# The heads' stage of a gated-linear-attention layer: DMAs, casts and evacuations in written order on every engine

## The chip, the cores and the metric

The kernel runs on one core of one Trainium2 chip. The metric is the device time of one execution in microseconds (us). The kernel before takes 2637.93 us, the median of three runs (2637.6 to 2638.26).

## What is computed

The reference is a two-layer step of a streaming encoder over 512 frames of one new stream (the prompt) and 16 frames each of eight running streams (the samples): 640 tokens of width 2048. Layer 0 is stick-breaking attention with a key and value cache, layer 1 is gated linear attention (GLA) with a recurrent state; both are preceded by a normalization with shift and scale from a condition, and gated. The change lies in layer 1, whose core is this chunk, run for four heads with DK = 256 and DV = 512:

```python
def gla_chunk(S, inp):
    q, k, v, g = inp                       # g = log of the decay, per token and key column
    b = jnp.cumsum(g, axis=1)
    b_last = b[:, -1]
    q_in = q * jnp.exp(b)
    a = jnp.einsum('bchd,bshd->bhcs', q_in, k * jnp.exp(-b))
    a = jnp.where(jnp.tril(jnp.ones((C, C), dtype=bool)), a, 0.0)
    o = jnp.einsum('bhcs,bshe->bche', a, v) + jnp.einsum('bchd,bhde->bche', q_in, S)
    S = jnp.exp(b_last)[..., None] * S + jnp.einsum('bshd,bshe->bhde', k * jnp.exp(b_last[:, None] - b), v)
    return S, o
...
g = jax.nn.log_sigmoid(a_lr @ w_a2 + b_a) / 16.0
o = o * lax.rsqrt(jnp.mean(o * o, axis=-1, keepdims=True) + EPS) * g_out
y = (o * jax.nn.silu(r)) @ w_out
```

The outputs are the encoded frames of both kinds, the new keys and values of layer 0, and the new states of layer 1: 4 of 256 x 512 for the prompt and 32 of them for the eight samples.

## The kernel before

Everything is float32. Large products are made of three products of halves: a value is split by `halves` (lines 134 to 136) into a rounded high part, cast on ScalarE (L135), and a low part, subtracted on VectorE (L136).

The stages follow one another: layer 0's condition and first values (to about 200 us), its input projections (L520, to 955), its attention (to 1450), its output product and layer 1's condition and first values (to 1700), layer 1's input projections (L520 again, to 2086), the heads' stage (lines 1288 to 1676, to 2510), and the last output products with the final norm (lines 1679 to 1748).

**The heads' stage** runs several strands side by side. TensorE's order is written out by the program (line 81), by a small clock `pe["now"]` that each matmul moves on. A strand is a generator, a *lane*; `step(wait, tp=n)` says that it goes on once that many microseconds of this clock have passed and n PSUM banks are free. Between pieces of the filler work, `side.tick()` (L305) runs the lanes that are due. The filler is first the plain projection of the queries and keys of heads 2 and 3 (`plain`, L575: 16 pieces of weights, 48 matmuls each), then two of the four groups of output products (`share`, L619: rows 0 to 3 and 4 to 7 of the gated output, times w_out). The lanes are:

- `decays` (L1397): for each head, loads q, k and the decay's weights, makes the cumulated log decays b on ScalarE and VectorE, and scales q and k by their exponentials. Two heads can be ready ahead.
- `prompt_lane` (L1451): 16 chunks of 128 tokens. For each: scores and turned keys kr (L1357, L1500), scores times values (`mm3`, L1345), queries times the state, which is scaled and split into S1h and S1l (L1472, L1473) once for each half of the key columns, then the norm (`normed`: L1369, the power on GpSimd L230, the scaling L1371), then the state's update. The turning back of the normalized chunk and its gating (`leave`, L1389, L1390) come in the next chunk.
- `sample_lane` (L1557): for each head, the eight samples at once. The keys times the decay (kd) are turned (L1585), split, stored to DRAM as two tiles (L1589) and read back by 12 loads of 16 rows x 4 x 128 (L1595) into kst, where high part, high part and low part stand below each other, 48 rows for each of two samples, so that one matmul of 128 rows makes the update of one sample (L1619). Then come four groups of four states: queries times states (L1613), four updates (L1619, L1621), and the states' stores.
- `fetches` (L1631): loads the gated rows of both lanes from DRAM, splits them (ogh, ogl) and so frees the output products to start: rows 0 to 13 here, 14 and 15 in the last stage.

**Who issues DMAs.** `load` and `store` go on SyncE's queue (L71, L74), `move` on GpSimd's (L78). Here SyncE has the weights, q, k, the values v and the rows; GpSimd has the state tiles s0 in and out (eight buffers, L1546, L1554), gates, values of the sample lane (vst), the plain projection's results, the gated results og, and the stacked keys. A DMA waits on its queue for what it reads or overwrites, and those behind it wait too.

**What sets the order.** In this stage only TensorE follows the program text. The order of VectorE, ScalarE, GpSimd and SyncE's queue is chosen at build time by a scheduler that simulates the program; in an earlier stage (lines 1161 to 1275) VectorE, ScalarE and GpSimd follow the text too.

## Time and profile before

| | us |
|---|---|
| median of three runs | 2637.93 |
| the profiled execution, its own time | 2633.23 |
| its span in the trace | 2631.4 |
| TensorE busy in the span | 2475.0 |
| VectorE busy | 1597.8 |
| ScalarE busy | 1017.4 |
| GpSimd busy | 261.3 |

The profile is of one execution. Its page gives busy times by engine; the windows give the same for a stretch of time, with TensorE's granted clock (1.00 is full speed), the mean busy share of the 16 DMA engines and their rate. In the list of waits, a row is the waiting engine, what it writes and its line, then what it waited for, the sum in us, the number of waits and the longest. "issue" is time in which nothing shows that the engine waited for. In the timeline, a row is the start, the time, the engine, line, instruction, what is written from what, its shape and how many; an idle time before it and its end are in brackets. PE is TensorE, PEld its weight loads, DVE VectorE, ACT ScalarE, POOL GpSimd, SPq SyncE's queue.

### The profile page before, as it was taken

What the parts mean: (1) busy time and instruction counts of PE and PEld (TensorE: products, weight loads), DVE (VectorE), ACT (ScalarE), POOL (GpSimd) and SP (SyncE); (2) the same over time, 40 slices, a digit from 0 to 9 for tenths busy, and PEclk for the clock granted to TensorE, in tenths of its full rate; (3) what the DMA queues carried; (4) which work ended last, traced back from release to release, by engine and by line L of the source; (5) the groups of instructions that cost most, each with busy time, mean ns of one, the idle gap of its engine ahead of it and who ended that gap; (6) DMA issues with size and microseconds to landing.
All of it is one profiled execution on the core that took longest, in us unless ns stands there. A gap on an engine that the chain in (4) does not pass through costs nothing.

```text
span 2631.4 us, 43839 instructions
## 1 busy us (share of the span) xinstructions
PE 2475.0 (94%) x17393; PEld 2162.9 (82%) x17393; DVE 1597.8 (61%) x2429; ACT 1017.4 (39%) x1804; POOL 261.3 (10%) x537
## 2 busy tenths in 40 slices
PE   6999999999999989999999989999999998787998
PEld 4569999989999989787777767999999987675776
DVE  4555556555556646766776666666677564555556
ACT  4332222222223335555453453333333362464333
POOL 1200000000000000000000050000000134424300
PEclk8899999999999999999999989999999998999999
DMA  9966666766674366666665633344543577846554
GB/s 314 314 208 222 216 216 202 232 209 216 198 237 144 118 215 212 227 209 221 209 225 173 189 110 108 90 119 117 144 119 105 170 226 233 280 158 209 203 196 148
DMA packets 495358, 503.83 MB, mean 191 GB/s; under 512 B 26090, under 2 KB 416626, under 8 KB 495026
## 3 DMA queue, kind: packets, MB, share of 16 engines
q1 hardware_dynamic: 477426, 446.49, 53.7%
q0 software_dynamic: 17728, 54.54, 6.3%
q8 instruction: 137, 2.24, 0.3%
q14 instruction: 67, 0.55, 0.1%
HBM read 411.16 MB, written 89.78 MB: 190 GB/s over the span
## 4 chain that ended last, share of the span: by engine, by line
PE 74%; DMA 7%; DVE 7%; issue 5%; ACT 3%; POOL 3%; SPq 1%; ACTq 0%; POOLq 0%; DVEq 0%
PE ps_mm L520 41%; PE ps_mm L619 8%; PE ps_mm L454 4%; PE ps_mm L356 3%; PE ps_mm L575 3%; PE ps_tp L976 2%; PE ps_tp L944 1%; PE ps_z L920 1%; PE ps_z L178 1%; DMA ar<-in_w_ada_dram 1%; PE ps_z L218 1%; DVE wl L136 1%; PE ps_tp L1021 1%; PE ps_mm L1747 1%; PE ps_z L989 1%
## 5 line engine op out<-in xcount | busy, mean ns | idle before, releaser
L520 PE MATMUL ps_mm<-sums,wh 128*128 128x320 f32 x2880 | 642.2, 311 | 0.4 <-ACT wh L135 0.4
L520 PE MATMUL ps_mm<-h,wh 128*128 128x320 f32 x2160 | 484.7, 313 | 5.5 <-ACT wh L135 3.8
L520 PEld LDWEIGHTS ps_mm<-sums,wh 128*128 128x128 f32 x2880 | 479.4, 188 | 12.2 <-issue 9.0
L520 PE MATMUL ps_mm<-sums,wl 128*128 128x320 f32 x1440 | 445.3, 309 | 0.7 <-DVE wl L136 0.7
L520 PEld LDWEIGHTS ps_mm<-h,wh 128*128 128x128 f32 x2160 | 360.4, 188 | 22.0 <-issue 13.3
L136 DVE TENSOR_TENSOR wl<-wr,wh 128x1024 fp32r<-128x1024 f32 x191 | 233.9, 1226 | 234.0 <-ACT wh L135 233.0
L135 ACT CAST wh<-wb 128x1024 fp32r<-128x1024 f32 x180 | 188.9, 1049 | 460.2 <-PE ps_mm L520 389.6
L520 PE MATMUL ps_mm<-h,wl 128*128 128x320 f32 x1080 | 334.8, 310 | 2.2 <-DVE wl L136 2.2
L135 ACT CAST wh<-wr 128x1024 fp32r<-128x1024 f32 x191 | 200.1, 1049 | 330.4 <-PE ps_mm L520 201.1
L520 PEld LDWEIGHTS ps_mm<-sums,wl 128*128 128x128 f32 x1440 | 270.4, 188 | 1.0 <-DVE wl L136 1.0
L136 DVE TENSOR_TENSOR wl<-wb,wh 128x1024 fp32r<-128x1024 f32 x180 | 219.9, 1222 | 66.0 <-ACT wh L135 63.4
L619 PE MATMUL ps_mm<-wh,ogh 128*128 128x512 f32 x450 | 199.7, 444 | 15.5 <-ACT ogh L135 11.0
L575 PE MATMUL ps_mm<-h,wh 128*128 128x320 f32 x896 | 209.1, 321 | 3.5 <-DVE out L526 2.1
L520 PEld LDWEIGHTS ps_mm<-h,wl 128*128 128x128 f32 x1080 | 203.5, 188 | 2.9 <-DVE wl L136 2.9
L619 PE MATMUL ps_mm<-wh,ogl 128*128 128x512 f32 x450 | 180.4, 401 | 0.6 <-DVE ogl L136 0.4
L619 PE MATMUL ps_mm<-wl,ogh 128*128 128x512 f32 x450 | 180.4, 401 | 0.0
L575 PEld LDWEIGHTS ps_mm<-h,wh 128*128 128x128 f32 x896 | 153.0, 193 | 16.0 <-issue 11.3
L575 PE MATMUL ps_mm<-h,wl 128*128 128x320 f32 x448 | 140.9, 315 | 2.3 <-DVE wl L136 2.3
L454 PE MATMUL ps_mm<-wh,h 128*128 128x512 f32 (+1 forms) x320 | 113.4, 425 | 10.0 <-ACT h L135 7.1
L619 PEld LDWEIGHTS ps_mm<-wh,ogh 128*128 128x128 f32 x450 | 87.8, 195 | 41.7 <-ACT ogh L135 12.2
L858 DVE TENSOR_TENSOR_SCAN k<-k,zero_c 128x544 f32<-128x544 f32 (+4 forms) x96 | 93.3, 975 | 29.7 <-ACT k L854 17.5
L619 PEld LDWEIGHTS ps_mm<-wh,ogl 128*128 128x128 f32 x450 | 86.6, 192 | 21.7 <-DVE ogl L136 1.8
(306 smaller groups left out, 3912.4 us busy)
## 6 DMA issues: line engine op xcount, KB each, us to landing
ar<-in_w_ada_dram SPq DMA_DIRECT2D x160, 512.0 KB
wb<-in_sb_w_in_dram SPq DMA_DIRECT2D x84, 512.0 KB
kc<-in_cache_sb_k_dram SPq DMA_DIRECT2D x64, 512.0 KB
vc<-in_cache_sb_v_dram SPq DMA_DIRECT2D x64, 512.0 KB
wb<-in_gla_w_in_dram SPq DMA_DIRECT2D x51, 512.0 KB
wr<-in_gla_w_in_dram SPq DMA_DIRECT2D x45, 512.0 KB
wr<-in_sb_w_in_dram SPq DMA_DIRECT2D x44, 512.0 KB
ar<-in_w_ada_dram SPq DMA_DIRECT2D x64, 256.0 KB
```

The source lines that it names most:

```text
L135: nc.scalar.copy(hi, x)
L136: dve.tensor_tensor(lo, x, hi.bitcast(F32), op=ALU.subtract)
L178: mm(acc[32 * q:32 * q + 32, :w], cT[:, kt + m, :], by(cT[:, kt + m, :], rs[m // each][:, m % each, q, :]), start=kt + m == 0, stop=kt + m ...
L218: mm(acc[32 * j:32 * j + 32, :256], cT[:, kt + m, :], by(cT[:, kt + m, :], r[:, 256 * j:256 * j + 256]), start=kt + m == 0, stop=kt + m == ...
L356: mm(acc[a], l[:, c], by(l[:, c], r[:, k2, :]), start=kt == k0 and first, stop=kt == k0 + nk - 1 and last)
L454: mm(acc[i][:n, :], l, by(l, r[:, e, :]), start=j == 0 and e == 0 and first, stop=j == 7 and e == 1 and last)
L520: mm(acc, l[:, k, :], by(l[:, k, :], r), start=start and k == 0 and first, stop=k == 7 and last, skip_group_check=True)
L575: mm(acc[nt], l[:, k, :], by(l[:, k, :], r), start=k0 == 8 and k == 0 and first, stop=k0 == 0 and k == 7 and last)
L619: mm(acc, l, by(l, r[:, e, :]), start=i == 0 and e == 0 and first, stop=i == 1 and e == 1 and last)
L858: dve.tensor_tensor_scan(kr, kr, zeros[:, :w], 1.0, ALU.mult, ALU.add)
L920: mm(z[:, :n], q[:, hh, qs], by(q[:, hh, qs], k[:, hh, :n]), start=True, stop=True)
L976: turn_block(tp[:, P * c:P * c + P], block(kc[:, c, P * hh:P * hh + P]), ident)
```

## The change

All but one of the edits are in the heads' stage.

1. VectorE, ScalarE, GpSimd and SyncE's queue follow the program text there (`manual_schedule`, closed behind the stage).
2. All of the stage's `move`s become `load`s: GpSimd's queue keeps only the power of the norm. State tiles have seven buffers for eight.
3. The stacked keys are no longer sent through DRAM. For half of the columns at a time, kd is written twice as high part and twice as low part beside each other (tile kc), turned in two transposes, and copied from PSUM to kst. The second half of the key columns (dt = 1) is made between the second and the third group of states.
4. In the prompt's lane, the next chunk's scores and turned keys are made before this chunk's products; the first half of the update stands between the two products with the state; the norm's scaling is a step later than its sum of squares and power.
5. The decays go in smaller steps, on whole rows of 640 instead of halves; the weights for the next head are loaded ahead; heads 2 and 3 need their own keys alone and not the whole plain projection.
6. The sample lane's values and gate are fetched at the end of the head before.
7. Waits (`step`, `side.after`) are set anew; rows 10 to 13 are loaded and split in the last stage.
8. In `plain`, and in `six`, which is used in earlier stages too, a weight piece is loaded one piece earlier than it is split; in `share` the next column's first piece is split after the first product of this one.

```diff
-S0 = 8
+S0 = 7
-    st_d = [[dp.tile([P, 256], F32, name=f"k_{h}_{d}") for d in range(2)] for h in range(GH)]
...
+    def wsplit(r, a):
+        return [t.rearrange("p (a n) -> p a n", a=a) for t in split(r)]
...
+        nxt, raw = wsplit(piece(0), 2), piece(1)
...
             if j < 7:
-                nxt = piece(j + 1)
+                nxt = wsplit(raw, 2)
+            if j < 6:
+                raw = piece(j + 2)
...
                 n0, k0, _ = todo[n]
-                return wpiece(src[:, k0:k0 + 8, n0:n0 + P], 8, P)
...
-                if nt == 0:
-                    nxt = piece(n + 1)
+                if nt == 0 and raw is not None:
+                    nxt, raw = wsplit(raw, 8), piece(n + 2)
+            if upper is not None and n == len(todo) - 2:
+                upper()
...
                 raws += [raw(c + 1, 0), raw(c + 1, 1)]
...
                     yield from products(acc, a, i, ws[i])
                 leave(a, c, acc)
+                if a == each[0] and c < 3:
...
-                    move(dst[:, hh, :], t[0])
+                    load(dst[:, hh, :], t[0])
+                    for h in (2, 3):
+                        if hh and dst is gk_d[h]:
+                            came.update(of=h, when=pe["now"])
...
+                                 for n0, dst in ((256 * h, gq_d[h]), (NK + 256 * h, gk_d[h])) for hh in range(2)],
+                       lambda: came.update(plain=True))
...
-            r = rstd_of(gl, s1, 512, "on")
+            return on, rstd_of(gl, s1, 512, "on"), o
+        def scaled_by(on, r, o):
             act(on, o, AF.Copy, scale=r)
             return on
...
-            move(g, gr_d[h][:, :, t0:t0 + P])
+            load(g, gr_d[h][:, :, t0:t0 + P])
...
-            move(og_d[h][:, :, t0:t0 + P], g)
+            load(og_d[h][:, :, t0:t0 + P], g)
...
-                while min(through.values()) < h - 1 or h >= 2 and not came["plain"]:
-                    yield step(0.5)
...
+            def weights(h):
+                r = gl.tile([96, 256], F32, tag="wa2r", name="wa2r", bufs=1)
-                load(q, gq_d[h])
-                load(k, gk_d[h])
                 yield step(4.0)
+                return wa2
+            wa2 = yield from weights(0)
+            for h in range(GH):
+                while min(through.values()) < h - 1 or h >= 2 and came["of"] < h:
+                    yield step(0.5)
+                if h >= 2:
+                    yield step(max(0.0, came["when"] + 5.0 - pe["now"]))
+                q, k = (gl.tile([P, 2, T], F32, tag=n, name=n, bufs=2) for n in ("q", "k"))
+                load(q, gq_d[h])
+                load(k, gk_d[h])
-                yield step(5.0)
+                yield step(1.0)
...
+                    yield step(0.8)
                     act(b, b, AF.Exp, scale=-1.0)
                     act(b, b, AF.Ln, bias=1.0)
+                    yield step(1.7)
                     dve.tensor_tensor(y, y, b, op=ALU.subtract)
                     dve.tensor_tensor_scan(b, reset, y, 0.0, ALU.mult, ALU.add)
+                    yield step(1.7)
...
+                    yield step(0.8)
                     for x, sign, f in ((q, 1.0, 1.0 / 16.0), (k, -1.0, 1.0)):
-                        for c in hs:
-                            e = gl.tile([P, HALF], F32, tag="e", name="e", bufs=1)
-                            act(e, b[:, c], AF.Exp, scale=sign * IT)
-                            dve.scalar_tensor_tensor(x[:, dt, c], x[:, dt, c], f, e, op0=ALU.mult, op1=ALU.mult)
-                    yield step(10.0)
+                        act(y, b, AF.Exp, scale=sign * IT)
+                        yield step(0.8)
+                        dve.scalar_tensor_tensor(x[:, dt], x[:, dt], f, y, op0=ALU.mult, op1=ALU.mult)
                 ready[h] = q, k, e1, el, ed, es
+                if h + 1 < GH:
+                    wa2 = yield from weights(h + 1)
...
+                side.after(5.0, lambda: fetch_gate(u + GP))
...
+            def scores(u):
...
                 a = attend(t0, k, q)
...
                 halves(*kr, tp[:, :256])
-                if c:
+                return a, kr
+            made, stored = None, 0.0
+            for u, (h, c) in enumerate(units):
+                while h not in ready:
+                    yield step(0.5)
+                    if left is not None:
+                        yield step(2.0, tp=1)
+                        leave_left()
+                q, k, e1, el, ed, _ = ready[h]
+                t0 = P * c
+                if made is None:
+                    yield step(0.0, tp=2)
+                    made = scores(u)
+                    yield step(2.0)
+                (a, kr), made = made, None
+                if c == 0:
+                    yield step(max(0.0, stored + 8.0 - pe["now"]))
+                    S = gl.tile([P, 2, 512], F32, tag="S", name="S")
+                else:
                     s1 = state(S, e1, 0, c)
                     qc = [gl.tile([P, 2, P], F32R, tag=n, name=n, bufs=1) for n in ("qch", "qcl")]
                     halves(*qc, q[:, :, t0:t0 + P])
+                if u + 1 < len(units) and units[u + 1][0] in ready:
+                    yield step(0.3, tp=2)
+                    made = scores(u + 1)
                 if left is not None:
-                    yield step(2.0, tp=1)
+                    yield step(0.3, tp=1)
                     leave_left()
-                    side.after(4.0, lambda u=u: fetch_gate(u - 1 + GP))
-                yield step(4.0, tp=1)
+                yield step(1.5, tp=1)
                 v = vs.pop(u)
...
-                    yield step(3.0)
-                    mm3(o, [x[:, 1, :] for x in qc], s1, False, True)
-                left = u, normed(o)
-                for dt in range(2):
-                    yield step(0.3, tp=1)
+                def update(dt):
...
+                yield step(0.3, tp=1)
+                update(0)
+                if c:
+                    yield step(1.5)
+                    mm3(o, [x[:, 1, :] for x in qc], s1, False, True)
+                on = normed(o)
+                yield step(0.3, tp=1)
+                update(1)
                 fetch(u + 2)
                 if c == 3:
-                    move(sp_o[0, 0, h].rearrange("(d p) v -> p d v", p=P), S)
-                yield step(0.5)
-            yield step(4.0, tp=1)
+                    load(sp_o[0, 0, h].rearrange("(d p) v -> p d v", p=P), S)
+                    stored = pe["now"]
+                yield step(1.0)
+                left = u, scaled_by(*on)
+            yield step(3.0, tp=1)
             leave_left()
...
-                move(s0, A["state_gla"][0, 2 * m + e, h, P * dt:P * dt + P, :])
+                load(s0, A["state_gla"][0, 2 * m + e, h, P * dt:P * dt + P, :])
...
-            move(ss_o[0, 2 * m + e, h, P * dt:P * dt + P, :], states.pop(x)[0])
-            side.after(8.0, ask)
+            load(ss_o[0, 2 * m + e, h, P * dt:P * dt + P, :], states.pop(x)[0])
+            side.after(5.0, ask)
...
+            def fetch(h):
...
-                        move(vst[r0:r0 + NT].bitcast(F32), rows)
+                        load(vst[r0:r0 + NT].bitcast(F32), rows)
+                return v, gate(h, NP, "gn", 1)
+            here = fetch(0)
+            for h in range(GH):
+                v, g = here
...
-                yield step(6.0, tp=1)
-                tp = bank("tp")
-                for dt in range(2):
-                    turn_block(tp[:, P * dt:P * dt + P], block(kd[:, dt, :]), ident)
-                khl = [gl.tile([P, 256], F32R, tag=n, name=n, bufs=2) for n in ("krh", "krl")]
-                halves(*khl, tp[:, :256])
-                for t, x in zip(st_d[h], khl):
-                    move(t, x.bitcast(F32))
-                def stack(e, dt):
-                    for i in range(3):
-                        rows = st_d[h][int(i == 2)][:, P * dt:P * dt + P].rearrange("(m e t) n -> e t m n", m=4, e=2)[e]
-                        r0 = 64 * e + NT * i
-                        move(kst[e][r0:r0 + NT].bitcast(F32), rows)
-                for e in range(2):
-                    stack(e, 0)
+                def stack(dt):
+                    for half in range(2):
+                        x = gl.tile([P, 256], F32R, tag="kc", name="kc", bufs=1)
+                        x4 = x.rearrange("p (s i t) -> p s i t", s=4, i=4)
+                        kx = kd[:, dt, 64 * half:64 * half + 64].rearrange("p (s t) -> p s t", s=4).unsqueeze(2)
+                        kx = kx.to_broadcast([P, 4, 2, NT])
+                        nc.scalar.copy(x4[:, :, 0:2], kx)
+                        dve.tensor_tensor(x4[:, :, 2:4], kx, x4[:, :, 0:2].bitcast(F32), op=ALU.subtract)
+                        yield step(1.5, tp=1 - half)
+                        tp = tp if half else bank("tp")
+                        for m in range(2):
+                            c = P * (2 * half + m)
+                            turn_block(tp[:, c:c + P], block(x.bitcast(F32)[:, P * m:P * m + P]), ident)
+                    for e in range(2):
+                        r = slice(64 * e, 64 * e + 48)
+                        (dve.tensor_copy if e else nc.scalar.copy)(kst[e][r], tp[r].rearrange("p (m n) -> p m n", m=4))
+                yield step(4.0)
+                yield from stack(0)
                 yield step(0.5, tp=1)
                 a = attend(NP, k, q)
-                yield step(5.0)
+                yield step(3.0)
...
-                since = pe["now"] + 9.0
+                since = pe["now"] + 1.0
...
-                    yield step(max(since, max(states[x][1] for x in group) + 7.0) - pe["now"], tiled=True)
+                    yield step(max(since, max(states[x][1] for x in group) + 6.5) - pe["now"], tiled=True)
...
-                        side.after(1.5, lambda x=group[m]: leaves(x))
-                    if n < 2:
-                        stack(e, 1)
+                        side.after(1.0, lambda x=group[m]: leaves(x))
+                    if n == 1:
+                        yield from stack(1)
+                        yield step(1.5)
                 on = normed(o)
-                yield step(8.0, tp=1)
+                yield step(2.5)
+                on = scaled_by(*on)
+                yield step(2.0, tp=1)
                 leave(h, NP, on, g)
                 through["s"] = h + 1
+                if h + 1 < GH:
+                    yield step(4.0)
+                    here = fetch(h + 1)
...
-            for kt in range(14):
+            for kt in range(10):
...
-                    yield step(2.0)
+                    yield step(5.0)
...
+        in_order = ExitStack()
+        in_order.enter_context(tc.manual_schedule(engines={mybir.EngineType.DVE, mybir.EngineType.Activation,
+                                                           mybir.EngineType.Pool, mybir.EngineType.SP}))
         for x in (decays(), prompt_lane(), sample_lane(), fetches()):
             side.add(x)
         drive(others)
-        came["plain"] = True
...
+        in_order.close()
...
-        for kt in (14, 15):
-            r = po.tile([P, T], F32, tag="rows", name="og_in", bufs=2)
-            load(r, og_d[3][:, kt - 12, :])
-            og1[kt] = [po.tile([P, T], F32R, name=f"og{n}{kt}") for n in "hl"]
+        for kt in range(10, 16):
+            r = po.tile([P, T], F32, tag="rows", name="og_in", bufs=6)
+            load(r, og_d[kt // 4][:, kt % 4, :])
+            n = 20 + 2 * kt % 12
+            og1[kt] = [slot(n + e) if kt < 14 else po.tile([P, T], F32R, name=f"og{e}{kt}") for e in range(2)]
             halves(*og1[kt], r)
```

45 lines of the change are left out of this document (16 added, 29 removed).

## The prediction

> **What bounds the kernel now.** I read the page first, then the windows by stage, then the waits inside the one stage that stands out, then its timeline. The page says that TensorE is busy 94% of the span.
>
> ```profile
> span 2631.4 us, 43839 instructions
> PE 2475.0 (94%) x17393; PEld 2162.9 (82%) x17393; DVE 1597.8 (61%) x2429; ACT 1017.4 (39%) x1804; POOL 261.3 (10%) x537
> ```
>
> The windows show where the other 6% are (columns: length, busy time of each engine, granted clock, DMA share, GB/s). In the first layer's projections (200 to 955) and the last products (2510 to 2593) TensorE has next to nothing to wait for. In the heads' stage, 2086.2 to 2510.4, it has.
>
> ```profile
> 200.00:955.00 755.00, 753.22 (x5649) 704.86 (x5648) 446.28 (x506) 216.68 (x247) 1.94 (x12) 1.00 0.62 196
> 2086.20:2283.00 196.80, 173.93 (x1048) 152.72 (x1048) 100.41 (x178) 86.39 (x165) 83.05 (x148) 0.94 0.78 245
> 2283.00:2510.40 227.40, 188.59 (x837) 142.96 (x837) 132.00 (x233) 110.10 (x206) 77.67 (x133) 0.92 0.57 193
> 2510.40:2593.00 82.60, 82.60 (x359) 67.46 (x360) 48.33 (x66) 24.69 (x41) 0.72 (x1) 1.00 0.61 199
> ```
>
> The stage takes 424.2 us. TensorE idles 22.9 + 38.8 = 61.7 us of it, while VectorE is busy 55% and the DMA engines 57 to 78%: no engine is full, they wait for each other. The waits of the stage name the places.
>
> ```profile
> POOL gate L78 <- issue: 40.6, 13, 5.8
> POOL out_dram L78 <- DVE s L1621: 35.4, 18, 9.9
> POOL og L78 <- DVE gate L1390: 32.4, 6, 8.2
> ACT on L1371 <- POOL on_r L230: 30.6, 7, 11.5
> PE ps_tp L1619 <- DMA kst<-k: 22.8, 3, 11.0
> PE ps_mm L619 <- ACT ogh L135: 8.7, 2, 7.8
> PE ps_tp L1389 <- ACT on L1371: 7.7, 4, 2.7
> PE ps_tp L1345 <- ACT S1h L1472: 5.9, 1, 5.9
> PE ps_z L1613 <- DMA s<-in_state_gla_dram: 5.3, 5, 2.0
> ```
>
> So TensorE's 61.7 us are 22.8 for stacked keys coming back from DRAM, 7.7 for the normalized chunk, 14.6 for ScalarE at the change from projections to output products (S1h and ogh), 5.3 for state loads, and 11.3 in waits of under 3 us each. Each idle stretch costs twice, as the granted clock shows: the first row is an idle of 1.62 us, the second the stretch after it, and the last the sum over all eight stretches of the stage at 0.50 or 0.51.
>
> ```profile
> 2148.36 0.64 PE L1619 MATMUL ps_tp<-vst,kst 128*128 128x512 f32 x1 [1.62 <-DVE gate L1390]
> 2148.50:2151.90 3.40, 3.40 (x13) 3.22 (x14) 2.60 (x5) 0.47 (x1) 1.30 (x2) 0.50 0.56 148
> sum 57.90, PE 34.93 PEld 28.18 DVE 27.67 ACT 16.92 POOL 21.80; mean PE 4.37 PEld 3.52 DVE 3.46 ACT 2.12 POOL 2.72
> ```
>
> TensorE worked 34.9 us at half clock, so it lost about 17.5 us more. What the stage can give back is 61.7 + 17.5 = 79 us.
>
> **The change part by part.** *Stacked keys.* The trip to DRAM and back ends: no store of krh and krl, no 12 row loads per head. TensorE, head 1's sample lane, before (L1585 turns kd, L1357 are scores; the keys are used behind the DMAs):
>
> ```order
> 7937 L1585 MATMUL ps_tp<-ident,kd 128x128 x2
> 7938 L575 MATMUL ps_mm<-h,wh 128x320 x2
> 7939 L575 MATMUL ps_mm<-h,wl 128x320
> 7940 L575 MATMUL ps_mm<-h,wh 128x320 x2
> 7941 L575 MATMUL ps_mm<-h,wl 128x320
> 7942 L1357 MATMUL ps_tp<-q,k 128x128 x2
> ```
>
> The same lane in the changed kernel (L1648 turns the stacked columns kc, L1356 updates the prompt's state):
>
> ```order
> 7973 L1648 MATMUL ps_tp<-ident,kc 128x128 x2
> 7974 L579 MATMUL ps_mm<-h,wh 128x320 x2
> 7975 L579 MATMUL ps_mm<-h,wl 128x320
> 7976 L579 MATMUL ps_mm<-h,wh 128x320 x2
> 7977 L579 MATMUL ps_mm<-h,wl 128x320
> 7978 L1356 MATMUL ps_tp<-v,krh 128x512 x2
> 7979 L1356 MATMUL ps_tp<-v,krl 128x512
> 7980 L579 MATMUL ps_mm<-h,wh 128x320 x2
> 7981 L579 MATMUL ps_mm<-h,wl 128x320
> 7982 L579 MATMUL ps_mm<-h,wh 128x320 x2
> 7983 L579 MATMUL ps_mm<-h,wl 128x320
> 7984 L1648 MATMUL ps_tp<-ident,kc 128x128 x2
> ```
>
> Two transposes per head become eight, in pairs with other work between, and the keys leave PSUM straight to their places. The wait goes: -22.8. The 24 added transposes cost 24 x 0.09 to 0.15 (four start within 0.36 us below): I take 0.11, +2.6. Their copies, subtractions and evacuations, each under half a microsecond, lie on engines that are half idle: 0.
>
> ```profile
> 2278.56 0.60 PE L1389 MATMUL ps_tp<-ident,on 128*128 128x128 f32 x4
> 2278.92 0.71 PE L1345 MATMUL ps_tp<-v,aTh 128*128 128x512 f32 x2
> ```
>
> *The norm.* GpSimd's power no longer stands behind stores that wait for VectorE, since every DMA leaves its queue, and the scaling is written a step later. Of 7.7 I take -6; bounds 0 and -7.7. *ScalarE at the change.* S1h no longer stands behind casts that wait for rows: 5.9. The ogh wait stays in part, because rows 2 and 3 are asked for and cast almost at once, now in fixed order: -9 of 14.6 together (bounds +5 and -14.6). *The small waits*: -6 of 11.3 (bounds +10, -11.3), by scores made a chunk ahead. *State loads*: seven buffers for eight, but the margin stays: 0 (bounds +5, -5.3).
>
> *The start.* Here the change adds a wait. SyncE's queue before, from alr to the fifth weight piece; four pieces are ahead of this:
>
> ```order
> 670 L71 DMA alr_in<-alr_d 96x640
> 671 L71 DMA wa2r<-in_gla_w_a_dram 16x256 x6
> 672 L71 DMA q<-gq_103 128x1280
> 673 L71 DMA k<-gk_107 128x1280
> 674 L71 DMA v<-gv_0_115 128x512
> 675 L71 DMA v<-gv_1_116 128x512
> 676 L71 DMA v<-gv_0_115 128x512
> 677 L71 DMA v<-gv_1_116 128x512
> 678 L71 DMA v<-gv_0_115 128x512
> 679 L71 DMA v<-gv_1_116 128x512
> 680 L71 DMA wr<-in_gla_w_in_dram 128x8x128
> ```
>
> The changed kernel's queue, the end of the same stretch; two pieces are ahead, and alr, seven states, six wa2r and four v stand above these rows:
>
> ```order
> 684 L71 DMA gate<-gr_103 128x4x128 x2
> 685 L71 DMA v<-gv_0_107 128x512
> 686 L71 DMA v<-gv_1_108 128x512
> 687 L71 DMA vst<-gv_0_107 16x4x512
> 688 L71 DMA vst<-gv_1_108 16x4x512
> 689 L71 DMA vst<-gv_0_107 16x4x512 x2
> 690 L71 DMA vst<-gv_1_108 16x4x512
> 691 L71 DMA vst<-gv_0_107 16x4x512
> 692 L71 DMA gate<-gr_103 128x4x128
> 693 L71 DMA wr<-in_gla_w_in_dram 128x8x128
> 694 L71 DMA q<-gq_95 128x1280
> 695 L71 DMA k<-gk_99 128x1280
> ```
>
> The third piece now stands behind 29 issues from alr on: 16 of states, gates and vst have come over from GpSimd's queue, q and k have moved behind it. The timeline of SyncE's queue and TensorE's first matmuls price it:
>
> ```profile
> 2089.37 0.84 SPq L71 DMA_DIRECT2D alr_in<-alr_d  x1
> 2090.27 7.84 SPq L71 DMA_DIRECT2D wa2r<-in_gla_w_a_dram  x6
> 2098.64 0.35 SPq L71 DMA_DIRECT2D q<-gq  x1
> 2103.11 0.39 SPq L71 DMA_DIRECT2D wr<-in_gla_w_in_dram  x1
> 2087.09 0.46 PE L575 MATMUL ps_mm<-h,wh 128*128 128x320 f32 x2
> 2087.53 0.46 PE L575 MATMUL ps_mm<-h,wh 128*128 128x320 f32 x2
> ```
>
> Fifteen issues took 13.7 us, 0.92 each; 29 take 27 us, so the piece is issued near 2116. TensorE has two pieces of 48 matmuls, three in 0.44 us: it needs the third at about 2102. That is a stall of 14 us, and up to 18 with landing and cast; nothing if the short issues go at the 0.35 us of an unhindered one. I take +8, between the ends, because the bytes ahead of it were also under way before. The Trainium skill, page "DMA: Bandwidth & Descriptors", section "Issuing engines are not separate DMA queues", says that DMAs of all engines share the same 16 engines and that issuing from several saves only sequencer time. By that rule this term is 0 and, with its clock share, the sum -53.6 instead of -43.4; the 7.84 us for six small issues speak against it.
>
> *The clock.* Idle left: 61.7 - 22.8 - 6 - 9 - 6 + 8 = 25.9, or 42%; so of the 17.5 us, 58% go: -10.2. The Trainium skill, "TensorE: Matmul & The Clock Gate", Part 1, lets the clock fall after an idle window of about 3.4 us, which would spare the short stalls this price; the 1.62 us idle above was followed by 3.4 us at 0.50, so the row decides. By the rule only the four long waits (two on kst, 7.8 and 5.9) cost 1.7 us each, 58% of 6.8 is 4.0, and the sum would be -37.2.
>
> *Elsewhere.* In the first stage a weight piece is now loaded one earlier than before; TensorE waits there for the condition's weights, so these come a little later and the piece a little earlier.
>
> ```profile
> PE ps_tp L178 <- DMA ar<-in_w_ada_dram: 12.5, 20, 1.6
> ```
>
> One such wait more or less is 1.6 us. The split made later in the output products changes nothing that TensorE waits for, and the four og rows that are cast at the last products fall into a window where TensorE is full and VectorE 59% busy. Together 0, bounds -2 and +6.
>
> The sum is -22.8 + 2.6 - 6 - 9 - 6 + 8 - 10.2 = -43.4 us. The profiled execution took 2633.2 us, 4.7 under the median of the three runs, 2637.93; I take the difference from the median: **2594.5 us**.
>
> **The rivals.** *Only the keys' wait goes*, the rest comes back under in-order queues: -22.8 + 2.6 + 8 - 17.5 x 14.8/61.7 = -16.4, 2621.5 us. For it: ScalarE and VectorE then also wait in order. *All waits go but the start*: -61.7 + 2.6 + 8 - 15.2 = -66.3, 2571.6. Against it: row loads and state loads keep their latency. *SyncE's queue becomes the bound.* It now carries every store, and a store that waits holds all loads behind it; the queue waited before too:
>
> ```profile
> SPq L71 <- PE ps_tp L1345: 139.9, 12, 23.9
> ```
>
> 316 issues at 0.35 are 111 us; 88 stores held 2.8 us each, the mean of the 24 waits of 67.8 us that GpSimd's stores had, are 246; with half of the 139.9 us for v buffers this is 427 us, with all of it 497. From 2.8 us per store on, the stage is thus no shorter than today's 424; midway, 462, it is 38 slower: 2676 us. The Trainium skill, same DMA page, "Anatomy of one DMA", says the semaphore wait sits on the issuing sequencer, which is what such a hold needs. Against it: v's loads are now written after the reads that free them.
>
> **How the numbers follow.** Forecast 0.53, only the keys 0.18, all waits 0.14, the queue 0.10, nothing measurable 0.05 (the keys' gain against an 18 us start leaves -3.6). A measurement of this kernel can tell about 0.2%, 5.3 us, from no change. Faster: 0.53 + 0.18 + 0.14 = 0.85; same 0.05; slower 0.10. The range leaves out the queue, the zero and a little of the best case: 2563 to 2626. The likeliest case alone spans 2575 to 2612.
>
> **What would show it.** Right: no wait of the stacked update on a DMA, no wait of ScalarE on the power above 2 us, idle of TensorE in the stage near 26 us, a stall of 5 to 15 us near 2100 on a cast of weights, less than half the time at half clock. Wrong: SyncE's queue waiting on stores for longer than on anything else while TensorE waits for weights or states, or VectorE waiting for ScalarE's casts in a row while TensorE idles.

## The result and the profile after

The changed kernel takes 2713.0 us (2707.4 to 2715.6, four runs) where the kernel before takes 2637.8 on the same chip: ratio 1.0287, interval 1.0266 to 1.0309. The forecast was 2594.5. It is 75 us slower, not 43 faster.

The profiled execution has a span of 2711.2 us against 2631.4, 79.8 more. The heads' stage lies at 2095.2 to 2588.9 now. So 9.0 us were lost ahead of it, 69.5 in it and 1.3 behind it. The page's first lines and the windows row of the stage (columns as before: length, busy time of each engine, granted clock, DMA share, GB/s):

```profile
span 2711.2 us, 43683 instructions
PE 2503.9 (92%) x17417; PEld 2179.9 (80%) x17417; DVE 1605.3 (59%) x2433; ACT 1020.9 (38%) x1808; POOL 111.3 (4%) x277
```

```profile
2095.20:2588.90 493.70, 389.59 (x1909) 310.34 (x1909) 242.96 (x420) 201.95 (x380) 11.03 (x20) 0.89 0.62 195
```

TensorE idles 493.7 - 389.6 = 104.1 us of the stage, where it idled 61.7. It is also busy 27 us longer for nearly the same matmuls, as the clock fell from 0.93 to 0.89. No other engine is near its limit: VectorE works 49% of the stage and ScalarE 41%. The waits of TensorE in the stage, and of SyncE's queue:

```profile
PE ps_z L1669 <- DMA s<-in_state_gla_dram: 33.0, 10, 5.9
PE ps_mm L625 <- ACT wh L134: 16.4, 2, 14.5
PE ps_tp L1403 <- ACT on L1385: 10.3, 2, 9.3
PE ps_mm L579 <- ACT pl L1316: 6.4, 1, 6.4
PE ps_tp L1368 <- DVE k L1470: 5.7, 2, 4.8
PE ps_mm L625 <- DVE wl L135: 5.6, 2, 3.1
```

```profile
SPq L71 <- DVE gate L1404: 94.1, 17, 10.9
SPq L71 <- DVE s L1677: 48.2, 21, 8.3
SPq L71 <- DVE wl L135: 24.8, 8, 8.7
```

The waits on kst are gone. In their place come the states, ten waits of 3.3 us on average, and ScalarE at the change to output products. SyncE's queue waits longest on stores: 94.1 us for gated results (17 og stores) and 48.2 for updated states (21 stores). This is the queue's state that the third rival named.

One held load in full, from the timeline of SyncE's queue and of the engines. ScalarE stands 9.71 us for TensorE and copies a result of the projection at 2219.26; the store of that result (gk) heads the queue until 2219.72; behind it come four state stores, of which two states had been ready since 2214.0 and 2215.4; the loads into their buffers go out from 2225.86, and TensorE stands for the last of them until 2232.38.

```profile
2216.94 0.72 ACT L1496 ACTIVATE S1h<-S,e 128x512 fp32r<-128x512 f32 x1 [9.71 <-PE ps_tp L1356]
2219.26 0.43 ACT L1316 COPY pl<-ps_mm 128x320 f32<-128x320 f32 x1
```

```profile
2213.26 0.74 DVE L1677 SCALAR_TENSOR_TENSOR s<-s,es,ps_tp 128x512 f32<-128x512 f32 x1
2214.63 0.75 DVE L1677 SCALAR_TENSOR_TENSOR s<-s,es,ps_tp 128x512 f32<-128x512 f32 x1 [0.62 <-PE ps_tp L1675]
```

```profile
2213.38 0.56 SPq L71 DMA_DIRECT2D og<-gate  x1
2219.72 0.34 SPq L71 DMA_DIRECT2D gk<-pl  x1
2220.16 0.55 SPq L71 DMA_DIRECT2D gate<-gr  x1
2220.80 2.12 SPq L71 DMA_DIRECT2D out_dram<-s  x4
...
2225.86 3.22 SPq L71 DMA_DIRECT2D s<-in_state_gla_dram  x4
```

```profile
2232.38 1.92 PE L1669 MATMUL ps_z<-s,qz 128*32 128x512 f32 x2 [5.86 <-DMA s<-in_state_gla_dram]
```

The change from projections to output products shows the same on ScalarE. It stands for og rows twice, 7.78 and 8.01 us, with the norm's scaling (L1385) behind the first and the casts of w_out (wh) behind the second. TensorE waits 9.34 and 14.46 us for just these two. The rows of the second stand were issued at 2371.53, behind 6.18 us of vst loads.

```profile
2361.60 0.73 ACT L134 CAST ogh<-og_in 128x640 fp32r<-128x640 f32 x1 [7.78 <-DMA og_in<-og]
...
2363.68 0.70 ACT L1385 ACTIVATE on<-ps_tp,on_r 128x512 f32<-128x512 f32 x1
...
2375.98 0.73 ACT L134 CAST ogh<-og_in 128x640 fp32r<-128x640 f32 x1 [8.01 <-DMA og_in<-og]
...
2378.91 1.99 ACT L134 CAST wh<-wr 128x1024 fp32r<-128x1024 f32 x2
```

```profile
2362.45 6.18 SPq L71 DMA_DIRECT2D vst<-gv  x6
2369.68 0.58 SPq L71 DMA_DIRECT2D gate<-gr  x1
2371.07 0.36 SPq L71 DMA_DIRECT2D s<-in_state_gla_dram  x1
2371.53 0.95 SPq L71 DMA_DIRECT2D og_in<-og  x2
```

```profile
2364.44 1.12 PE L1403 MATMUL ps_tp<-ident,on 128*128 128x128 f32 x4 [9.34 <-ACT on L1385]
2380.01 0.79 PE L625 MATMUL ps_mm<-wh,ogh 128*128 128x512 f32 x1 [14.46 <-ACT wh L134]
```

### The profile page after: what moved, and what is told of

It is laid out like the page before. It is cut to its first block, busy times and chain, and to the rows that moved or that the text cites. A ratio compares the mean times of both kernels' runs of the same rounds, so it can differ in the third digit from the quotient of the medians.

```text
span 2711.2 us, 43683 instructions
## 1 busy us (share of the span) xinstructions
PE 2503.9 (92%) x17417; PEld 2179.9 (80%) x17417; DVE 1605.3 (59%) x2433; ACT 1020.9 (38%) x1808; POOL 111.3 (4%) x277
## 4 chain that ended last, share of the span: by engine, by line
PE 73%; DMA 10%; DVE 8%; ACT 3%; issue 2%; SPq 2%; POOL 0%; ACTq 0%; DVEq 0%; POOLq 0%
PE ps_mm L524 39%; PE ps_mm L625 8%; PE ps_mm L458 4%; PE ps_mm L579 4%; PE ps_mm L358 3%; SPq L71 2%; PE ps_tp L983 2%; DMA s<-in_state_gla_dram 2%; DVE wl L135 1%; PE ps_tp L1356 1%; PE ps_tp L951 1%; PE ps_z L927 1%; PE ps_z L220 1%; PE ps_z L180 1%; PE ps_z L996 1%
## 5 line engine op out<-in xcount | busy, mean ns | idle before, releaser
L524 PE MATMUL ps_mm<-sums,wh 128*128 128x320 f32 x2880 | 644.0, 312 | 10.4 <-ACT wh L134 10.4
L524 PE MATMUL ps_mm<-h,wh 128*128 128x320 f32 x2160 | 484.7, 312 | 6.7 <-ACT wh L134 3.6
L524 PEld LDWEIGHTS ps_mm<-h,wh 128*128 128x128 f32 x2160 | 360.2, 188 | 23.1 <-issue 13.3
L579 PE MATMUL ps_mm<-h,wh 128*128 128x320 f32 x896 | 217.3, 330 | 8.6 <-ACT pl L1316 6.4
L625 PE MATMUL ps_mm<-wh,ogh 128*128 128x512 f32 x450 | 199.6, 444 | 20.7 <-ACT wh L134 16.4
L625 PE MATMUL ps_mm<-wl,ogh 128*128 128x512 f32 x450 | 180.4, 401 | 5.6 <-DVE wl L135 5.6
L625 PE MATMUL ps_mm<-wh,ogl 128*128 128x512 f32 x450 | 179.8, 400 | 0.4 <-DVE ogl L135 0.4
L579 PEld LDWEIGHTS ps_mm<-h,wh 128*128 128x128 f32 x896 | 159.1, 201 | 24.7 <-issue 14.4
L625 PEld LDWEIGHTS ps_mm<-wh,ogh 128*128 128x128 f32 x450 | 87.2, 194 | 48.9 <-ACT wh L134 17.2
L625 PEld LDWEIGHTS ps_mm<-wh,ogl 128*128 128x128 f32 x450 | 86.6, 192 | 20.8 <-DVE ogl L135 0.9
```

Source lines behind the costliest of these rows:

```text
L524: mm(acc, l[:, k, :], by(l[:, k, :], r), start=start and k == 0 and first, stop=k == 7 and last, skip_group_check=True)
L579: mm(acc[nt], l[:, k, :], by(l[:, k, :], r), start=k0 == 8 and k == 0 and first, stop=k0 == 0 and k == 7 and last)
L625: mm(acc, l, by(l, r[:, e, :]), start=i == 0 and e == 0 and first, stop=i == 1 and e == 1 and last)
```

## The experiments

The kernel before took 2627.9 to 2637.8 us on the chips of these runs, so each run is compared by its ratio to the kernel before on its own chip. The stage's length and TensorE's idle time in it are from one profiled execution of each run, so differences of some 5 us between stages show little; the stage of the changed kernel, run twice, took 493.7 and 491.9 us.

| run | ratio | interval | stage us | idle us |
|---|---|---|---|---|
| before | 1 | | 424.2 | 61.7 |
| changed | 1.0287 | 1.0266-1.0309 | 493.7 | 104.1 |
| nothing written (e1) | 0.9932 | 0.9917-0.9947 | 399.3 | 40.5 |
| SyncE's queue free (e2) | 1.0089 | 1.0072-1.0106 | 436.1 | 71.3 |
| SyncE's queue alone written (e7) | 1.0191 | 1.0165-1.0218 | 462.0 | 78.1 |
| VectorE alone written (e10) | 1.0032 | 1.0018-1.0046 | 421.8 | 62.5 |
| ScalarE alone written (e11) | 0.9992 | 0.9980-1.0004 | 417.8 | 56.4 |
| stores on GpSimd (e5) | 1.0232 | 1.0212-1.0252 | 472.3 | 94.2 |
| all moves on GpSimd (e6) | 1.0343 | 1.0318-1.0369 | 500.9 | 118.5 |
| stores written later (e19) | 1.0248 | 1.0222-1.0274 | 476.0 | 98.8 |
| rows cast later, queue free (e17) | 1.0031 | 1.0018-1.0043 | 422.9 | 52.5 |
| six as before (e3) | 1.0289 | 1.0274-1.0305 | 496.8 | 106.8 |
| keys alone on before (e4) | 0.9855 | 0.9828-0.9881 | 385.3 | 29.8 |
| keys, one queue (e12) | 0.9870 | 0.9853-0.9887 | 389.6 | 33.9 |
| keys, og and gates on SyncE (e18) | 0.9882 | 0.9868-0.9897 | 389.4 | 35.4 |
| keys, scores ahead (e14) | 0.9931 | 0.9907-0.9955 | 398.2 | 41.5 |
| keys, scores ahead, one queue (e15) | 0.9934 | 0.9919-0.9949 | 402.4 | 46.4 |
| nothing written, six as before (e8) | 0.9908 | 0.9885-0.9930 | 401.2 | 40.6 |
| the same, moves on GpSimd (e9) | 1.0003 | 0.9989-1.0017 | 423.2 | 58.2 |

**The written order.** e1 takes the manual schedule out of the changed kernel's stage (below); e2 takes out SyncE's queue alone, by leaving `mybir.EngineType.SP` out of the set. The expectation of e1 names three theories, A, B and C, to which the later runs refer.

```diff
-        in_order = ExitStack()
-        in_order.enter_context(tc.manual_schedule(engines={mybir.EngineType.DVE, mybir.EngineType.Activation,
-                                                           mybir.EngineType.Pool, mybir.EngineType.SP}))
...
-        in_order.close()
```

> Everything of the change stays except the written order of VectorE, ScalarE, GpSimd and SyncE's queue, which the scheduler chooses again. Theory A (the one in-order SyncE queue holds state loads and weights behind stores that wait) and theory B (the written order of VectorE and ScalarE puts waiting casts of weights ahead of the lanes' work) both expect the stage's +69.5 us to go nearly all: TensorE's 33.0 us of waits on states under 10, and a time of 2640 to 2655, the 8.6 us of the first stage left. Theory C (the new plan of the lanes, its short margins and seven state buffers, is to blame whatever the order) expects 2690 to 2715.

> VectorE, ScalarE and GpSimd keep the written order; SyncE's queue alone is ordered by the scheduler. Theory A expects most of the stage's excess to go: 2645 to 2670, state waits under 12 us. Theory B expects little: 2690 to 2715, with the 14.5 us stall at the change to output products and the ScalarE waits still there.

Without the written order the same plan is 18.7 us faster than the kernel before, more than any of the three expected: theory C falls. With SyncE's queue alone freed, 57.6 of the 94.4 us between the two stages come back, and the state waits fall from 33.0 us to 5.2:

```profile
PE ps_z L1669 <- DMA s<-in_state_gla_dram: 5.2, 2, 2.8
```

The other 36.8 us stay: so A and B each have a part. What e2 still shows is the stall at the change: ScalarE stands 10.41 us at the cast of a row (second line below), then come the norm's scaling and S1h.

```profile
2310.66 0.94 ACT L1445 ACTIVATE b<-ps_tp,cols 128x320 f32<-128x320 f32 x2
2322.01 0.72 ACT L134 CAST ogh<-og_in 128x640 fp32r<-128x640 f32 x1 [10.41 <-DMA og_in<-og]
2322.64 0.68 ACT L1385 ACTIVATE on<-ps_tp,on_r 128x512 f32<-128x512 f32 x1
```

In e1, where the scheduler chose the order, the longest waits of TensorE in the stage are these, and none on a state is over 1.6 us:

```profile
PE ps_tp L1368 <- DVE k L1470: 6.3, 1, 6.3
PE ps_mm L625 <- DVE y L630: 5.9, 3, 5.2
PE ps_tp L1444 <- DVE wa L1420: 5.2, 1, 5.2
```

**One engine written at a time.** e7, e10 and e11 keep one name of the set (`{SP}`, `{DVE}`, `{Activation}`).

> The change with SyncE's queue alone in written order; VectorE, ScalarE and GpSimd are ordered by the scheduler. With the queue freed the stage fell from 493.7 to 436, and with everything freed to 399. If queue and engines add, the queue alone makes 399 + 57 = 456 and about 57 us over the run with no written order. If the queue's written order only hurts because in-order engines deliver its stores late, it makes 400 to 425 here. If the queue alone is to blame and the engines' order is harmless, 480 to 494.

> The change with VectorE alone in written order. The stage takes 399 us with no written order and 436 with VectorE, ScalarE and GpSimd written. If ScalarE's order makes those 37 us (it stands 10.4 us at a cast of og rows that are not there yet, with the norm's scaling behind it), VectorE alone costs 0 to 12: a stage of 399 to 411. If VectorE's does, 425 to 436.

> The change with ScalarE alone in written order. If a cast of og rows or weights that heads ScalarE's order is what costs, the stage takes 425 to 436 us, with a stall of TensorE of 8 us or more at the change to output products. If the two engines only hold each other when both are written, both this run and the one with VectorE alone stay under 411.

The queue alone gives 462.0, nearest to the 456 of adding, and the state waits are all there:

```profile
PE ps_z L1669 <- DMA s<-in_state_gla_dram: 35.0, 10, 5.5
```

VectorE alone costs 22.5 and ScalarE alone 18.5; neither expectation had that. Each puts work on og rows that are not there yet ahead of what TensorE needs. VectorE stands 6.80 us at a row's low half, and TensorE waits 17.5 us at a split of w_out (wl) behind it; ScalarE stands 6.65 us at the cast of a row, and TensorE waits 8.6 us at the norm's scaling.

```profile
PE ps_mm L625 <- DVE wl L135: 20.1, 2, 17.5
```

The two costs add: 41.0 of the stage against 36.8 with VectorE, ScalarE and GpSimd written, and by the ratios, which rest on all runs, 26 + 16 = 42 us against 41. That leaves next to nothing for GpSimd, which was not written alone. The queue's 62.7 (by the ratios 68) with these 36.8 (41) is a little more than the 94.4 (93) of all four, so queue and engines share at most a small part.

**What is held in the queue.** e5 and e6 keep everything in written order, but put the waiting stores, or all of the stage's moves, back on GpSimd's queue. The first diff is e5's in its four places (e6 does it with s0, vst and the gates too), the second e19's, which writes the stores later:

```diff
-                    load(dst[:, hh, :], t[0])
+                    move(dst[:, hh, :], t[0])
...
-            load(og_d[h][:, :, t0:t0 + P], g)
+            move(og_d[h][:, :, t0:t0 + P], g)
...
-                    load(sp_o[0, 0, h].rearrange("(d p) v -> p d v", p=P), S)
+                    move(sp_o[0, 0, h].rearrange("(d p) v -> p d v", p=P), S)
...
-            load(ss_o[0, 2 * m + e, h, P * dt:P * dt + P, :], states.pop(x)[0])
+            move(ss_o[0, 2 * m + e, h, P * dt:P * dt + P, :], states.pop(x)[0])
```

```diff
-            load(og_d[h][:, :, t0:t0 + P], g)
+            side.after(4.0, lambda: load(og_d[h][:, :, t0:t0 + P], g))
...
-                        side.after(1.0, lambda x=group[m]: leaves(x))
+                        side.after(5.0, lambda x=group[m]: leaves(x))
```

> All engines and SyncE's queue stay in written order, but the stores that wait for an engine (updated states, the prompt's state, gated results og, results of the plain projection) go back on GpSimd's queue; loads stay on SyncE's. Theory A (a waiting store holds the loads behind it) expects the state waits of 33.0 us to fall to 5 to 15 and the time to 2650 to 2680. Theory B expects 2695 to 2715. A price against both: the norm's power on GpSimd stands behind stores again (7.7 us of TensorE's waits before).

> The change in written order throughout, but states in and out, gates, vst, og and the projection's results on GpSimd's queue, as before the change. If one queue for all is the trouble, two in-order queues give 40 to 70 us of the stage back (ratio 1.00 to 1.012), at the price of the norm's power behind stores. If any queue in written order is held by its own stores and buffers, little changes: ratio 1.018 to 1.03, state waits over 20 us.

> The change in written order throughout, with the updated states' stores and the og stores written 4 us of the program's clock later; the plan's length stays. If stores written ahead of their data hold SyncE's queue, its waits on VectorE (94.1 us for gates of og, 48.2 for states) fall by half and the time falls by 15 to 40 us against the changed kernel (ratio to the kernel before 1.014 to 1.023 instead of 1.029). If the queue is held as long by its other waits, the waits on VectorE fall but the states still come late: ratio 1.024 to 1.035, with 25 us or more of state waits, since each state is also asked for 4 us later.

e5 and e19 do what theory A says, by less than it says. With the stores on the other queue the state waits fall to 19.4 us and the stage by 21. Written later, they fall to 19.1 and the stage by 18, and the queue's wait for gates from 94.1 to 17.5, though not that for states (53.1). The ratio of e19, 1.0248, lies where its rival had it, so most of the loss is left. The queue's own rows in e19:

```profile
SPq L71 <- DVE s L1677: 53.1, 28, 9.4
SPq L71 <- DMA og<-gate: 42.6, 16, 6.1
SPq L71 <- DVE wl L135: 28.7, 9, 6.9
SPq L71 <- ACT pl L1316: 28.1, 6, 10.1
SPq L71 <- PE ps_tp L1675: 21.7, 4, 10.9
SPq L71 <- DVE gate L1404: 17.5, 7, 9.6
```

The next waits take over: on projection results, on weight buffers (wl). In e5, where the stores have left the queue, the loads that need them hold it in their place: those that wait for a state's store, which frees its buffer, and those that wait for an og store.

```profile
SPq L71 <- DMA out_dram<-s: 101.0, 25, 17.4
SPq L71 <- DMA og<-gate: 71.3, 12, 12.8
```

So no single kind of store is the cause: in both runs the queue, still in written order, waits at whatever heads it next. e6 shows that two queues are no cure: 1.0343, with 34.6 us of state waits, and the norm's power behind GpSimd's stores (ScalarE's scaling waits 31.7 us for it, and TensorE's L1403 24.4 us for the scaling). The Trainium skill, page "DMA: Bandwidth & Descriptors", section "Issuing engines are not separate DMA queues", says that a second issuing engine saves only time on the sequencer. e6 agrees; the 21 us of e5 came with 13.6 us less of state waits, that is by what stands behind what on a queue.

**Margins.** e16 altered one number, the 6.5 us of the plan's clock between a state's load and its use, to 12; e17 altered the time between asking for og rows and their cast, on e2.

```diff
-                    yield step(max(since, max(states[x][1] for x in group) + 6.5) - pe["now"], tiled=True)
+                    yield step(max(since, max(states[x][1] for x in group) + 12.0) - pe["now"], tiled=True)
...
-                    yield step(4.0)
+                    yield step(12.0)
```

> The change as it is, all in written order, with one number altered: a group of states is used 12 us of the program's clock after its last load was written, not 6.5; TensorE does filler in between and the plan is no longer. If the state waits (33.0 us) come from a margin that the held queue overruns by 3 to 6 us each time, they fall under 12 and the time falls by 25 to 45 us (2670 to 2690 against 2713). If the queue only slips further, because TensorE's own waits hold the stores, the waits stay above 20 and the time within 12 us of the changed kernel.

The edit moved no instruction, so the run is a second one of the changed kernel (1.0288, 1.0272 to 1.0304). That tells one thing: in the plan every group is already used at least 12 us behind its load, and the chip still had TensorE wait ten times, 3.3 us on average. So a margin longer than the plan's own was not tried.

> The change with SyncE's queue ordered by the scheduler (2650.7 us, stage 436), and og rows cast 12 us of the program's clock after they are asked for, not 4. If the cast of rows that are not there stands at the head of ScalarE's order and holds the norm's scaling and S1h, the stalls of 12.4 and 6.3 us at the change to output products go, and the stage falls by 10 to 22 us to 414 to 426. If the rows come late because og itself is late, the stall stays at 10 us or more and the stage at 430 to 445.

The stage fell by 13.2 us to 422.9, as expected, but only one of the two stalls went: the waits of L625 on wh and y fell from 15.0 to 4.6 us, and one of 9.6 us on the norm's scaling stayed. In it ScalarE stands for a row for 2.29 us only; most of the time it works on what is written ahead of the scaling. So rows are not all of ScalarE's share.

**The other parts.** e3 takes the edit in `six` back; e8 does so without the written order, and e9 has GpSimd's moves as well.

```diff
-        nxt, raw = wsplit(piece(0), 2), piece(1)
+        nxt = piece(0)
...
-                nxt = wsplit(raw, 2)
-            if j < 6:
-                raw = piece(j + 2)
+                nxt = piece(j + 1)
```

> Only the edit in six is taken back: in the earlier stages a weight piece is loaded when it is split, not one earlier. In the changed kernel TensorE waits 10.4 us at 184.4 us for a cast of a weight piece, and its first stages end 9 us later than before. If that edit alone did it, the time falls by 8 to 10 us to 2703 to 2705 and the heads' stage stays as long (493.7 us). If the wait comes from something else (the condition's weights being late in any case), nothing changes: 2713.

> No written order of VectorE, ScalarE, GpSimd and SyncE's queue, and six as before. The run without written order was 18.7 us under the kernel before; the earlier load in six cost 8.4 us up to the first plain projection. The two should add: 25 to 29 us under the kernel before. If the earlier load also helps in the second layer's condition, some of the 8.4 us comes back: 19 to 25.

> As the run with no written order and six as before, but states in and out, gates, vst, og and the projection's results go on GpSimd's queue again. If one scheduled queue holds loads behind stores, two queues gain another 3 to 10 us. If the norm's power behind waiting stores is what a DMA on GpSimd costs (7.7 us of TensorE's waits before), it is 3 to 10 us slower than that run, with the waits of L1403 on ScalarE back.

The changed kernel's wait of 10.4 us at 184.4 goes in e3, and the first plain projection starts at 960.4 us, not 969.8. The cause is SyncE's queue in the first stage: three weight pieces of the next projection are issued at 172.50, behind the values' stores, where the kernel before issues them at 164.47.

```profile
164.47 2.48 SPq L71 DMA_DIRECT2D wb<-in_sb_w_in_dram  x3
```

```profile
172.50 2.46 SPq L71 DMA_DIRECT2D wb<-in_sb_w_in_dram  x3
```

```profile
PE ps_mm L524 <- ACT wh L134: 10.4, 1, 10.4
```

The whole time of e3 does not show it: 2705.1 us, and 2705.6 for the changed kernel on the same chip (e16), since e3's heads' stage was 5 us longer in its profile. The start of the stage does, over all profiles: with the edit in `six` the heads' stage begins at 2087.9 to 2096.0 us (eleven), without it at 2081.1 to 2086.2 (nine), 7.7 us earlier on average. e8 is 24.6 us under the kernel before, 6.3 more than e1 by the ratios, though their intervals meet. So the edit costs about 8 us ahead of the stage and 0 to 6 in all.

e9 is 26 us slower than e8, where neither expectation had more than 10: TensorE waits 10.2 us on states, 9.8 on the norm's scaling and 8.7 on scaled keys. Under this plan one scheduled queue is better than two.

**The keys alone**, on the kernel before, with seven state buffers (e4; `stack` and the rest as in the change's diff, in place of the stores and loads of the keys). e12 makes a `load` of every `move` of the stage, e18 of those for og and gates; e14 takes over `prompt_lane` and the split `normed`, e15 both that and the loads:

```diff
-S0 = 8
+S0 = 7
...
+                yield step(4.0)
+                yield from stack(0)
...
+                    if n == 1:
+                        yield from stack(1)
+                        yield step(1.5)
```

> The kernel before with one part of the change: the stacked keys made by transposes, with seven state buffers. The prediction's step expects the 22.8 us of waits on kst to go, 2.6 us of transposes to come, and about 6 us of half-clock time to go with the idle: 20 to 27 us under the kernel before on this chip. A rival says that the wait only moves: with the keys there earlier TensorE meets the next late thing, the states (now 5.3 us, with a buffer less) or ScalarE; then 0 to 10 us under it, and the waits on states grow by 10 us or more.

> The kernel before with stacked keys by transposes and with all of the stage's DMAs on SyncE's queue, ordered by the scheduler. Moving them so was worth 22 us of the stage under the change's plan (423 to 401). If that gain belongs to the queue (GpSimd's stores hold its loads and the norm's power), it comes here too: 12 to 25 us under the run with the keys alone (stage 360 to 373). If it belongs to the change's plan only, or if two queues are better where the plan fits them, 0 to 15 us over it (stage 385 to 400).

> The kernel before with stacked keys by transposes, and with the stores of og and the loads of gates on SyncE's queue; states, vst and the projection's results stay on GpSimd's. With the keys alone the stage takes 385 us, 4.5 of it TensorE's wait for the scaled norm and 5.4 for states. If the og stores on GpSimd's queue (they wait for VectorE) hold the norm and the states, both waits shrink: 375 to 383. If SyncE's queue then holds q, k, v or rows behind og, 386 to 400.

> The kernel before with stacked keys by transposes and the change's order in the prompt's lane: scores one chunk ahead, half of the update between the two products with the state, the scaling a step later. The stage takes 385 us without this part, and 423 with the whole new plan on the same queues. If scores made ahead cost it (masks and casts of the next chunk stand before this chunk's), 400 to 425; if the decays in small steps, the row waits and the state margins do, 380 to 392.

> Stacked keys by transposes and the change's prompt lane (scores ahead) on the kernel before, and all of the stage's DMAs on SyncE's queue as the scheduler orders it. With GpSimd's queue this plan waits 16.8 us for the scaled norm and its stage takes 398 us. If that wait is the norm's power behind stores on GpSimd, it goes under 4 and the stage falls to 375 to 385. If the later scaling itself makes it late, the wait stays over 10 and the stage at 392 to 405.

The keys alone bring 38.6 us (2589.3 against 2627.9), more than expected and the lowest ratio of all versions, though the intervals of e12 and e18 meet its own. The stage's row and its longest waits:

```profile
2085.20:2470.50 385.30, 355.46 (x1909) 293.37 (x1909) 236.42 (x431) 200.97 (x391) 132.62 (x225) 0.96 0.73 233
```

```profile
PE ps_z L1616 <- DMA s<-in_state_gla_dram: 5.4, 2, 4.7
PE ps_mm L619 <- DVE y L624: 4.9, 1, 4.9
PE ps_tp L1389 <- ACT on L1371: 4.5, 2, 3.0
```

Idle fell by 31.8 us: the 22.8 on kst, and 9 more that nothing in the edit aims at (S1h and ogh at the change to output products, 14.6 before, are 3.5). Busy time fell by 7.0 with the clock. Nothing added to it gains. All DMAs on one queue, and og and gates there, each lengthen the stage by 4 us, which is within the noise; scores ahead cost 13, and with one queue 17. So the gain from one queue (e8 against e9) does not carry over to this plan. In e14 the wait for the norm's scaling is 16.8 us, and e15, without GpSimd's queue, keeps 12.0 of it: so most of it is not the queue. That the later scaling makes it was expected so, but not tried by itself.

## Why the prediction was wrong

The forecast was 43 us faster and the result is 75 us slower. The step that failed is that the sum has no term for the written order itself, on SyncE's queue and on the engines; only its rivals name it.

The stage, split along the runs (profiled executions, so good to some 5 us): 424.2 before; keys alone -38.9; the rest of the plan on the old queues (e9) +37.9; all DMAs on SyncE's queue under the scheduler (e8) -22.0, with the load in six (e1) -1.9; VectorE, ScalarE and GpSimd written (e2) +36.8; SyncE's queue written +57.6; 493.7.

*The keys, -22.8 + 2.6.* Right: the wait went, and in e4, where they come alone, nothing took its place. There they bring more than the step said.

*The start, +8.* Near in size, by luck. The piece was issued at 2117.07, forecast near 2116, and the stall was 6.4 us against 8.

```profile
2117.07 0.40 SPq L71 DMA_DIRECT2D wr<-in_gla_w_in_dram  x1
2123.80 0.90 PE L579 MATMUL ps_mm<-h,wh 128*128 128x320 f32 x2 [6.38 <-ACT pl L1316]
```

But the stage begins 9.0 us later than in the trace that the step was read from. The 29 issues from alr (2098.32) on took 18.8 us, 0.65 each, not 27; and TensorE, which stood 4.3 us for the decays' weights (wa2, at 2108.9), was through with its two pieces at 2117.4, not 2102. So the 6.4 us are the piece's landing, its cast (ScalarE waits 6.3 us for it) and the copy of pl behind that, and none of the 14 us that the step laid on the queue. The 4.3 us and 4.8 more for scaled keys (k, at 2144.1) were not foreseen. They stay in e1 (5.2 and 6.3) and, with moves on GpSimd, in e9 (4.0 and 8.7), while e4 has 1.0 and no such wait on k: they belong to the new plan, not to the order or the queue. Which of its steps makes them was not tried.

*ScalarE at the change, -9 of 14.6, and the norm, -6 of 7.7.* Failed. The step saw that rows 2 and 3 are cast in fixed order right after they are asked for, and left 5.6 us for it; it should have asked what stands behind those casts on ScalarE. The norm's scaling and the casts of w_out do, and 9.3 + 14.5 + 3.1 us came of it. That the norm no longer stands behind stores was true, and it was late all the same.

*State loads, 0 with bounds +5 and -5.3.* Failed, the largest term: 33.0 us against 5.3. The step looked at the number of buffers; what counted was the queue in which the loads stand (5.2 with it freed in e2, 35.0 with it alone written in e7).

*SyncE's queue as the bound*, a rival at 0.10 with 2676 us. This is the nearest of the cases: its sign, its place and what would show it (the queue waiting on stores longest while TensorE waits for states). Its sum is not how the time was lost, though. It asked for 2.8 us for each of 88 stores; the og stores that waited held 5.5 each (94.1 over 17) and the state stores 2.3 (48.2 over 21), and with the prompt's states (9.7 over 7) that is 152.0 us, 1.7 per store, at which, with its other terms, the sum says no loss. What counted was which loads stood behind a store when TensorE needed them, as in the timeline above. And the rival has no term for the engines, whose written order costs 36.8 us beside the queue's 57.6. The Trainium skill, page "PSUM — Partial Sum Buffer", section "Engine vs sequencer instructions", says of the queues of ScalarE, VectorE and GpSimd that they "are strict FIFO"; the trace agrees: in e2 the norm's scaling, written behind a cast, came only after the 10.41 us at that cast.

*The small waits, -6, and elsewhere, 0.* Both failed. Scores ahead lost 13 us where tried alone (e14). The load in six moved three weight pieces behind stores and made one wait of 10.4 us, where the bound was +6.

*The clock, -10.2.* The rule (time at half clock goes with idle time) held in direction, with the sign turned round: idle up by 42.4, busy time up by 27.1. In size it did not: by the step's proportion, 17.5 us for 61.7 of idle, 42.4 more would cost 12.0, and without the 2.6 us of added transposes busy time rose by 24.5.

Most of the error lies in one choice. Chances of 0.85 for faster rested on TensorE's waits that the change aims at; the scheduler's order, which the waits of the trace of before were measured under, was taken to be no better than the written one. It was better by 94 us of the stage, of some 118 between the forecast and the result. Of the plan's +37.9 on the old queues, scores ahead explain about 13; which of the decays, margins and row waits make the rest was not tried apart and stays open.

## What to carry to other kernels

A written order on an engine or a queue is only as good as the clock that it was written by: for each operation that may come late (a cast of loaded rows, a store of a result), look at what stands behind it in that order, because that is late as well. Before fixing an order, run the same program with the order left to the scheduler; here that one run separates a loss of 75 us from a gain of 19. And a change in many parts deserves its parts one at a time: the one that removed the longest named wait, alone, beat both kernels by 38 us and more.

## What the runs showed of the hardware

The time at half clock follows the idle time of TensorE over all runs. From the windows' mean clock, taken as a mix of 1.00 and the 0.50 that the single stretches of the trace before show, the stage of the changed kernel was at half clock for 2 x 0.11 x 493.7 = 109 us with 104.1 of idle; of e2, 2 x 0.07 x 436.1 = 61 with 71.3; of e4, 2 x 0.04 x 385.3 = 31 with 29.8; the furthest off is e17, 2 x 0.08 x 422.9 = 68 with 52.5. What that costs is read from TensorE's busy time for nearly the same matmuls: 355.5 us in e4 and 389.6 in the changed kernel, 34.1 more for 74.3 us more of idle. So, as an estimate from these two, an idle microsecond in this stage, where idles are mostly 1 to 10 us, costs about one and a half: itself, and nearly half of another in slower matmuls. Single runs stray from that: e6 has 382.4 us of busy time with 118.5 of idle, e7 383.9 with 78.1.
